# Gate and up products of a decoder's feed-forward: the high part of the weights meets both parts of x in one 512-column product

## Chip, core and metric

The kernel is one program on one NeuronCore of a Trainium2 chip. The metric is the time of one execution on the device in microseconds (us), lower is better. Engines are named as the profile names them: PE is TensorE's matmul, PEld its weight load, DVE is VectorE, ACT is ScalarE, POOL is GpSimd, SP is the queue that issues the DMAs.

## What is computed

Four decoder layers over 256 positions of width 1024. Each layer is a token mixer plus cross-attention, an output projection, a LayerNorm, and then a SwiGLU feed-forward of inner width 2816 with a second LayerNorm. The change is in the feed-forward alone:

```
def swiglu(x, w_gate_up, w_down):
    g, u = jnp.split(x @ w_gate_up, 2, axis=-1)
    return (jax.nn.silu(g) * u) @ w_down
...
        x = layer_norm(ALPHA * x + mixed, ln1_g[i], ln1_b[i])
        x = layer_norm(ALPHA * x + swiglu(x, w_gate_up[i], w_down[i]), ln2_g[i], ln2_b[i])
```

All inputs are float32.

## The kernel before

**Three products for one.** Each float32 operand is held as two parts of type fp32r: a high part (the value cast to fp32r) and a low part (the value minus its high part). A product of two operands is then the sum of high times high, high times low and low times high, all added into one PSUM bank. `mm3` issues these three matmuls (lines 256, 257 and 258), each with a weight load of its own (PEld).

**Weights.** They arrive in halves of 128 x 1024 float32 (512 KB) in the order of a plan. SP loads a half into one of four `raw` buffers (line 206), ACT casts it to the high part `wh` (line 214), DVE or POOL subtracts to the low part `wl` (line 230 or 228). In the feed-forward all but the first few low parts are DVE's. There are six pairs of `wh` and `wl`; a pair is free again once the last matmul that reads it is done, and a `raw` buffer once the low part is made.

**The feed-forward.** The 2816 inner columns are 22 blocks of 128. Blocks 0 and 1 are made another way (`a_mode`) and are not touched. Each of the other 20 is a *unit* in this text: `gu(i)` calls `t_mode`, which keeps the weights in the array and streams x transposed (`xT`, the high part `xh` and the low part `xl`, each 128 x 8 x 256). A unit uses two halves of weights; for the gate columns (`c` = 0) and then the up columns (`c` = 1) it runs 8 steps of k with `mm3`, so 2 x 8 x 3 = 48 matmuls of 256 columns. Gate and up lie side by side in one PSUM bank. Over four layers there are 80 units.

`t_task` reads the unit: silu of the gate on ACT (line 1057), times up on DVE (line 1059), the high part of the result `fth` on ACT (line 1061), the low part `ftl` on DVE (line 1063). It has three `sil` buffers to work in, one for a unit.

`down` multiplies the 128 positions of a row block with the rows of `w_down`: per block of inner columns 2 row blocks x 2 halves of columns x 3 matmuls of 512 columns, added into four PSUM banks that stay taken for the whole feed-forward. Four of the eight banks are left for units.

**Order.** PE's order is that of the program; the other engines' instructions are placed by a scheduler. In the middle of a feed-forward PE goes round a *period*: two units (block 2j+3, then 2j+4; called A and B here), then two blocks of `down` (2j+2 and 2j+3), 24 matmuls of 512 columns. So the first block of a `down` is the B of the period before, the second is this period's A. A period uses six halves of weights, two for A, two for B, one for each block of `down`, which is one round of the six pairs. At the end of a layer five units come one after another, then the last blocks of `down` (17 to 21 in `finish`), and the LayerNorm.

Of the kernel before, what the change touches and what calls it, by code (L numbers as in the profile page):

```python
# [10 lines left out]
F32R = mybir.dt.float32r  # L11
BF = mybir.dt.bfloat16
I32 = mybir.dt.int32
AF = mybir.ActivationFunctionType
OP = mybir.AluOpType
# [3 lines left out]
S = 256  # L19
# [19 lines left out]
def weight_plan():  # L39
    plan = []  # L40
    for l in range(DEPTH):
        kind = KINDS[l]
        v = [("v", l, i) for i in range(3)]
        qk = [("qk", l, i) for i in range(6)]
        if kind == 0:
            qi, qm = [("qi", l, 0), ("qi", l, 1)], ("qm", l, 0)
            if l:
                plan += [*qi, v[0], qk[0], qm, qk[1], v[1], qk[2], qk[3], qk[4], v[2], qk[5]]
            else:
                plan += [*qi, v[0], qm, qk[0], qk[1], v[1], qk[2], qk[3], qk[4], qk[5], v[2]]  # L50
                i = plan.index(MEM_AT)
                plan[i:i] = [("mk", 0, 0), ("mv", 0, 0)]
        elif kind == 1:
            plan += [v[0], qk[0], ("qm", l, 0), qk[2], v[1], qk[4], qk[1], qk[3], qk[5], v[2]]
        else:
            plan += [v[0], qk[0], ("qm", l, 0), qk[1], v[1], qk[2], qk[3], v[2], qk[4], qk[5]]
        plan += [("out", l, i) for i in (3, 0, 1, 2)]
        if l + 1 < DEPTH:
            plan += [("mk", l + 1, 0)]
        plan += [("gu", l, i) for i in range(3)]  # L60
        for j in range(NFF // 2):
            plan += [("dn", l, j)] + [("gu", l, i) for i in (2 * j + 3, 2 * j + 4) if i < NFF]
        plan.remove(("dn", l, NFF // 2 - 3))
        plan.remove(("dn", l, NFF // 2 - 2))
        i = plan.index(("dn", l, NFF // 2 - 1))
        plan[i:i] = [("dn", l, NFF // 2 - 3), ("dn", l, NFF // 2 - 2)]
        if l + 1 < DEPTH:
            plan += [("mv", l + 1, 0)]
    return plan
# [16 lines left out]
class Slots:  # L86
    def __init__(self, items):
        self.free = list(items)
# [24 lines left out]
class K:  # L113
    def __init__(self, tc, io, ctx):
        self.tc, self.nc, self.io = tc, tc.nc, io
        pool = lambda n: ctx.enter_context(tc.tile_pool(name=n, bufs=1))
        self.sb = pool("sb")
        self.pp = ctx.enter_context(tc.tile_pool(name="ps", bufs=1, space=bass.MemoryType.PSUM))

        ctx.enter_context(tc.manual_schedule(engines={mybir.EngineType.PE}))  # L120
        self.stalls = {}
        self.tasks = []
        T = self.t
        pair = lambda shp, tag, n: Slots([(T(shp, F32R, f"{tag}h{i}"), T(shp, F32R, f"{tag}l{i}")) for i in range(n)])
        one = lambda shp, tag, n, dt=F32: Slots([T(shp, dt, f"{tag}{i}") for i in range(n)])
        self.banks = Slots([self.pp.tile([128, 512], F32, name=f"bank{i}") for i in range(8)])
        self.raws = one([128, HALF], "raw", NR)
        self.cvs = pair([128, HALF], "w", NB)
        self.nats = one([128, 256], "nat", 3)
        self.qs = one([128, 2, 128], "q", 4, F32R)  # L130
        self.qms = one([128, 2, S], "qm", 2, F32R)
        self.es = {128: one([128, 2, 128], "e", 3), 256: one([128, 2, 256], "E", 3)}
        self.pTs = {1: pair([128, 1, 2, 128], "pa", 2), 2: pair([128, 2, 2, 128], "pb", 2)}
        self.vs = pair([128, 2, 256], "v", 3)
        self.fts = pair([128, S], "ft", 8)
        self.sils = one([128, S], "sil", 3)
        self.kks = one([128, 2, 2, S], "k", NKB, F32R)
        self.sts = one([128, 64], "st", 12)
        self.xT = (T([128, 8, S], F32R, "xh"), T([128, 8, S], F32R, "xl"))
        self.memT = (T([128, 8, S], F32R, "mh"), T([128, 8, S], F32R, "ml"))  # L140
        self.mk = [T([128, 2, 2, S], F32R, f"mk{i}") for i in range(2)]
        self.mv = (T([128, 2, 256], F32R, "mvh"), T([128, 2, 256], F32R, "mvl"))
        self.x = [T([128, D], F32, f"x{tb}") for tb in range(2)]
        self.lng, self.lnb = T([128, D], F32, "lng"), T([128, D], F32, "lnb")
        self.plan = weight_plan()
        self.hv = parts(self.plan)
        self.h0 = {}
        for i, (n, h, _) in enumerate(self.hv):
            if h == 0:
                self.h0[self.plan[n]] = i  # L150
        self.raw, self.cv = {}, {}
        self.n_raw = self.n_hi = self.n_lo = 0
        self.edge = False
# [137 lines left out]
    def t_mode(self, xT, key):  # L291
        b = self.take(self.banks, "bank")
        p = b.rearrange("p (c t) -> p c t", c=2)
        for c in range(2):
            for k in range(8):
                w = self.half(key, k // 4)
                cs = slice((k % 4) * 256 + c * 128, (k % 4) * 256 + c * 128 + 128)
                self.mm3(p[:, c], (w[0][:, cs], w[1][:, cs]), (xT[0][:, k], xT[1][:, k]), k == 0, k == 7)
                if k % 4 == 3:
                    if c:  # L300
                        self.free_half(key, k // 4)
                    if not (c and k == 7):
                        self.tick()
        return b, p

    def down(self, accs, what, l, kb, tb, ft, first):
        ts = slice(tb * 128, tb * 128 + 128)
# [727 lines left out]
    def ffn(self, l, ts):  # L1035
        nc = self.nc
        fts = [None] * NFF
        for i in range(N_AMODE):
            fts[i] = self.take(self.fts, "ft")
        gut = {}  # L1040

        def a_task(i, tb, b):
            s = yield from self.tk(self.sils)
            nc.scalar.activation(s[:, 0:128], b[:, 0:128], AF.Silu)
            nc.vector.tensor_tensor(s[:, 0:128], s[:, 0:128], b[:, 128:256], op=OP.mult)
            self.banks.put(b)
            yield W_A
            q = yield from self.tk(self.banks)
            nc.tensor.transpose(q[:, 0:128], s[:, 0:128], self.ident)
            t = slice(tb * 128, tb * 128 + 128)  # L1050
            self.split((fts[i][0][:, t], fts[i][1][:, t], q[:, 0:128], None))
            self.banks.put(q)
            self.sils.put(s)

        def t_task(i, b, p):
            s = yield from self.tk(self.sils)
            nc.scalar.activation(s, p[:, 0], AF.Silu)
            yield 1
            nc.vector.tensor_tensor(s, s, p[:, 1], op=OP.mult)  # L1059
            self.banks.put(b)  # L1060
            nc.scalar.copy(fts[i][0], s)  # L1061
            yield 1
            nc.vector.tensor_tensor(fts[i][1], s, fts[i][0], op=OP.subtract)
            self.sils.put(s)

        for tb in range(2):
            self.join(ts[tb])
            for i in range(N_AMODE):
                b = self.a_mode(self.xT, tb, ("gu", l, i), tb == 1)
                gut[i, tb] = self.spawn(a_task(i, tb, b))  # L1070
                self.tick()
        accs = self.new_accs()
        self.edge = False
        self.ln_params("ln2", l)

        def gu(i):
            b, p = self.t_mode(self.xT, ("gu", l, i))
            fts[i] = self.take(self.fts, "ft")
            gut[i, 0] = gut[i, 1] = self.spawn(t_task(i, b, p))
            self.tick()  # L1080

        def ready(kb, tb):
            self.join(gut[kb, tb])

        stop = NFF - HOLD_DN
        for what, _, i in [p for p in self.plan if p[1] == l and p[0] in ("gu", "dn")]:
            if what == "gu":
                if i >= N_AMODE:
                    gu(i)
                continue  # L1090
            for kb in (2 * i, 2 * i + 1):
                if kb < stop:
                    for tb in range(2):
                        ready(kb, tb)
                        self.down(accs, "dn", l, kb, tb, fts[kb], kb == 0)
                    self.fts.put(fts[kb])
        ts = self.finish(accs, "dn", l, range(stop, NFF), fts, ready, False, l == DEPTH - 1)
        for f in fts[stop:]:
            self.fts.put(f)
        return ts  # L1100
# [100 lines left out]
```

## Time and profile before

| | |
|---|---|
| median of 3 runs | 1353.04 us (1347.6 to 1353.33) |
| the profiled execution | 1351.82 us, span of its trace 1350.0 us, mean granted clock 0.983 |
| PE busy | 1287.3 us (95% of the span), 9186 matmuls |
| DVE busy | 897.5 us (66%) |
| ACT busy | 762.9 us (57%) |
| POOL busy | 316.4 us (23%) |
| read from memory | 223.02 MB, 166 GB/s over the span |

The span runs from the first to the last instruction in the trace; 1.82 us of the profiled execution lie outside it. Busy times of matmuls overlap on PE (each lasts longer than the distance to the next), so a busy PE says that it had work, and the distance from start to start says how fast it went.

### The profile page before, as it was taken

To read this page: it belongs to the slowest core of one execution; us is meant where nothing else is said; L and a number is where in the kernel's file an instruction comes from. 1 tells how busy PE (TensorE), PEld (TensorE's weight loads), DVE (VectorE), ACT (ScalarE), POOL (GpSimd) and SP (SyncE) were. 2 spreads that over 40 slices of the span, in tenths; PEclk is the share of its full clock that TensorE was granted. 3 is DMA by queue.
4 is the path that set the end of the run, shared out by engine and by line. 5 is a ranking of instruction groups with operands and counts; after the bars stand their busy time and mean duration, and the time that the engine had idled before them with its cause. 6 is when DMAs were issued, how large, how long until landed. Compare 5 with 4: busy or idle time off the path is not lost. (4 is left out here: it accounts for less than half of the span.)

```text
span 1350.0 us, 24249 instructions
## 1 busy us (share of the span) xinstructions
PE 1287.3 (95%) x9186; PEld 1212.5 (90%) x9186; DVE 897.5 (66%) x1940; ACT 762.9 (57%) x1512; POOL 316.4 (23%) x277
## 2 busy tenths in 40 slices
PE   6889899999999789999999999999999899999997
PEld 5879799999999779999989989999999898899996
DVE  7887775555578886555567877555568997655555
ACT  5668754444469745444447986444445897544441
POOL 3434440000045343000034444000014533300000
PEclk9989999999999889999999999999999999999999
DMA  8443356556564136565545345666546333655551
GB/s 300 126 149 110 110 180 199 187 188 184 170 203 150 70 103 240 185 189 180 183 155 180 133 141 169 206 185 188 186 138 218 127 125 126 203 188 188 187 176 59
DMA packets 63190, 225.65 MB, mean 167 GB/s; under 512 B 7776, under 2 KB 7776, under 8 KB 63072
## 3 DMA queue, kind: packets, MB, share of 16 engines
q1 hardware_dynamic: 62784, 224.10, 50.2%
q8 instruction: 72, 1.18, 0.4%
q14 instruction: 46, 0.38, 0.1%
q10 hardware_dynamic: 288, 0.00, 0.0%
HBM read 223.02 MB, written 1.05 MB: 166 GB/s over the span
## 5 line engine op out<-in xcount | busy, mean ns | idle before, releaser
L214 ACT CAST wh<-raw 128x1024 fp32r<-128x1024 f32 (+1 forms) x402 | 420.8, 1048 | 318.6 <-PE bank L257 177.2
L230 DVE TENSOR_TENSOR wl<-raw,wh 128x1024 fp32r<-128x1024 f32 (+1 forms) x294 | 378.2, 1288 | 273.9 <-ACT wh L214 269.1
L228 POOL TENSOR_TENSOR wl<-raw,wh 128x512 fp32r<-128x512 f32 x216 | 296.7, 1399 | 727.7 <-ACT wh L214 718.2
L256 PE MATMUL bank<-xh,wh 128*128 128x256 f32 x1344 | 382.1, 284 | 0.0
L257 PE MATMUL bank<-xl,wh 128*128 128x256 f32 x1344 | 381.2, 284 | 0.0
L258 PE MATMUL bank<-xh,wl 128*128 128x256 f32 x1344 | 381.2, 284 | 0.0
L257 PEld LDWEIGHTS bank<-xl,wh 128*128 128x128 f32 x1344 | 258.6, 192 | 1.2
L256 PEld LDWEIGHTS bank<-xh,wh 128*128 128x128 f32 x1344 | 258.6, 192 | 1.3
L258 PEld LDWEIGHTS bank<-xh,wl 128*128 128x128 f32 x1344 | 258.5, 192 | 0.0
L256 PE MATMUL bank<-wh,xh 128*128 128x256 f32 (+1 forms) x768 | 228.5, 298 | 2.8 <-ACT wh L214 1.9
L257 PE MATMUL bank<-wl,xh 128*128 128x256 f32 (+1 forms) x768 | 221.6, 289 | 2.5 <-DVE wl L230 2.3
L258 PE MATMUL bank<-wh,xl 128*128 128x256 f32 (+1 forms) x768 | 221.7, 289 | 0.8 <-DVE xl L270 0.6
L256 PE MATMUL bank<-wh,fth 128*128 128x512 f32 x480 | 189.8, 395 | 0.4 <-ACT fth L265 0.4
L257 PE MATMUL bank<-wl,fth 128*128 128x512 f32 x480 | 188.2, 392 | 0.0
L258 PE MATMUL bank<-wh,ftl 128*128 128x512 f32 x480 | 188.0, 392 | 0.0
L256 PEld LDWEIGHTS bank<-wh,xh 128*128 128x128 f32 x768 | 150.1, 196 | 4.0 <-ACT wh L214 2.4
L257 PEld LDWEIGHTS bank<-wl,xh 128*128 128x128 f32 x768 | 150.1, 195 | 3.1 <-DVE wl L230 3.1
L258 PEld LDWEIGHTS bank<-wh,xl 128*128 128x128 f32 x768 | 149.9, 195 | 1.7 <-DVE xl L270 1.7
L258 PEld LDWEIGHTS bank<-wh,ftl 128*128 128x128 f32 x480 | 90.5, 189 | 19.9 <-DVE ftl L270 0.7
L256 PEld LDWEIGHTS bank<-wh,fth 128*128 128x128 f32 x480 | 90.7, 189 | 17.5 <-ACT fth L265 0.8
L257 PEld LDWEIGHTS bank<-wl,fth 128*128 128x128 f32 x480 | 90.7, 189 | 16.3
L1061 ACT CAST fth<-sil 128x256 fp32r<-128x256 f32 x80 | 32.5, 406 | 107.3 <-DVE sil L1059 107.3
(194 smaller groups left out, 1553.0 us busy)
## 6 DMA issues: line engine op xcount, KB each, us to landing
raw<-in_w SPq DMA_DIRECT2D x396, 512.0 KB, 3.9
lng<-in_ln_g SPq DMA_DIRECT2D x8, 512.0 KB, 4.0
lnb<-in_ln_b SPq DMA_DIRECT2D x8, 512.0 KB, 6.2
raw<-in_w SPq DMA_DIRECT2D x4, 492.0 KB, 4.8
x<-in_xT SPq DMA_DIRECT2D x2, 512.0 KB, 5.4
E<-in_mem SPq DMA_DIRECT2D x4, 256.0 KB, 5.6
x<-in_x SPq DMA_DIRECT2D x2, 512.0 KB, 6.0
out_x<-x SPq DMA_DIRECT2D x4, 256.0 KB, 2.2
```

The costliest lines, as they stand in the source:

```text
L214: self.nc.scalar.copy(c[0][:, 0:wd], self.raw[n][:, 0:wd])
L228: self.nc.gpsimd.tensor_tensor(lo[:, c], r[:, c], hi[:, c], op=OP.subtract)
L230: self.nc.vector.tensor_tensor(lo[:, 0:wd], r[:, 0:wd], hi[:, 0:wd], op=OP.subtract)
L256: mm(out, lhsT=ah, rhs=bh, start=first, stop=False)
L257: mm(out, lhsT=ah, rhs=bl, start=False, stop=False)
L258: mm(out, lhsT=al, rhs=bh, start=False, stop=last)
L1061: nc.scalar.copy(fts[i][0], s)
```

## The change

The two parts of x now lie in one tile `x2`, 128 x 8 x 2 x 256, so that for each k the high part's 256 columns are followed by the low part's. `xT` names the two parts as slices of it for all other uses. A unit is made by `wide_mode` in place of `t_mode`: it takes two PSUM banks, one for gate and one for up. For each of them and each half of the weights it issues four matmuls of 512 columns, the weights' high part with both parts of x, and then four of 256 columns, the weights' low part with x's high part, into the first 256 columns of the bank. That is 2 x 2 x (4 + 4) = 32 matmuls in place of 48. The reader now has to add the two halves of each bank: an ACT copy of the second half, a DVE add of the first half to it, for gate and for up; then silu, the product and the two parts as before. A unit's reader takes two of the three `sil` buffers.

```
-        self.xT = (T([128, 8, S], F32R, "xh"), T([128, 8, S], F32R, "xl"))
+        self.x2 = T([128, 8, 2, S], F32R, "x2")
+        self.xT = (self.x2[:, :, 0], self.x2[:, :, 1])
...
+    def wide_mode(self, key):
...
+        mm = self.nc.tensor.matmul
+        bs = [self.take(self.banks, "bank") for _ in range(2)]
+        for c in range(2):
+            for h in range(2):
+                w = self.half(key, h)
+                cs = [slice(k * 256 + c * 128, k * 256 + c * 128 + 128) for k in range(4)]
+                for k in range(4):
+                    mm(bs[c], lhsT=w[0][:, cs[k]], rhs=self.x2[:, 4 * h + k].rearrange("p a t -> p (a t)"),
+                       start=h == k == 0, stop=False)
+                for k in range(4):
+                    mm(bs[c][:, 0:S], lhsT=w[1][:, cs[k]], rhs=self.x2[:, 4 * h + k, 0], start=False, stop=h == 1 and k == 3)
+                if c:
+                    self.free_half(key, h)
+                if not (c and h):
+                    self.tick()
+        return bs
...
-        def t_task(i, b, p):
+        def t_task(i, bs):
             s = yield from self.tk(self.sils)
-            nc.scalar.activation(s, p[:, 0], AF.Silu)
+            u = yield from self.tk(self.sils)
+            for d, b in ((s, bs[0]), (u, bs[1])):
+                nc.scalar.copy(d, b[:, S:2 * S])
+                nc.vector.tensor_tensor(d, b[:, 0:S], d, op=OP.add)
+                self.banks.put(b)
+            nc.scalar.activation(s, s, AF.Silu)
             yield 1
-            nc.vector.tensor_tensor(s, s, p[:, 1], op=OP.mult)
-            self.banks.put(b)
+            nc.vector.tensor_tensor(s, s, u, op=OP.mult)
+            self.sils.put(u)
             nc.scalar.copy(fts[i][0], s)
...
-            b, p = self.t_mode(self.xT, ("gu", l, i))
+            bs = self.wide_mode(("gu", l, i))
```

How the instructions stand on PE, in a unit of the first layer. First the kernel before, around the step from a unit's first half of weights (`wh_77`, `wl_78`) to its second (`wh_79`, `wl_80`); a row is one matmul with its output, its two inputs and its size:

```order
L256 MATMUL bank_65<-xh,wh_77 128x256
L257 MATMUL bank_65<-xl,wh_77 128x256
L258 MATMUL bank_65<-xh,wl_78 128x256
L256 MATMUL bank_65<-xh,wh_79 128x256
L257 MATMUL bank_65<-xl,wh_79 128x256
L258 MATMUL bank_65<-xh,wl_80 128x256
```

The same engine after the change, at the end of a `down` and through the first five groups of an A (x4 is four in a row; `x2` is printed as x_150):

```order
L257 MATMUL bank_64<-wh_83,fth_126 128x512
L258 MATMUL bank_64<-wl_84,fth_126 128x512
L259 MATMUL bank_64<-wh_83,ftl_127 128x512
L317 MATMUL bank_65<-x_150,wh_85 128x512 x4
L320 MATMUL bank_65<-x_150,wl_86 128x256 x4
L317 MATMUL bank_65<-x_150,wh_75 128x512 x4
L320 MATMUL bank_65<-x_150,wl_76 128x256 x4
L317 MATMUL bank_69<-x_150,wh_85 128x512 x4
```

Units and blocks of `down` follow one another as before; within a unit each high part of the weights is now loaded into the array once for both parts of x, and its low part is first read after four products.

ACT in one period of the first layer, before; the two readers are those of blocks 13 (its result `fth_126`) and 14 (`fth_128`):

```order
L214 CAST wh_81<-raw_72 128x1024
L214 CAST wh_83<-raw_73 128x1024
L214 CAST wh_85<-raw_74 128x1024
L214 CAST wh_75<-raw_71 128x1024
L1057 ACTIVATE sil_133<-bank_67 128x256
L1061 CAST fth_126<-sil_133 128x256
L214 CAST wh_77<-raw_72 128x1024
L214 CAST wh_79<-raw_73 128x1024
L1057 ACTIVATE sil_134<-bank_70 128x256
L1061 CAST fth_128<-sil_134 128x256
```

ACT in the same period after the change (gate banks 65 and 70, up banks 69 and 67):

```order
L1080 COPY sil_133<-bank_65 128x256
L1083 ACTIVATE sil_133<-sil_133 128x256
L215 CAST wh_85<-raw_74 128x1024
L215 CAST wh_75<-raw_71 128x1024
L1080 COPY sil_132<-bank_69 128x256
L1087 CAST fth_126<-sil_133 128x256
L1080 COPY sil_134<-bank_70 128x256
L215 CAST wh_77<-raw_72 128x1024
L1083 ACTIVATE sil_134<-sil_134 128x256
L215 CAST wh_79<-raw_73 128x1024
L1080 COPY sil_132<-bank_67 128x256
L1087 CAST fth_128<-sil_134 128x256
```

The six casts of the weights keep their order among themselves; the readers' pieces now stand between them, the gate's copy and silu ahead of the casts that follow its unit's weights, the up's copy behind them.

DVE at the same place after the change:

```order
L1081 TENSOR_TENSOR sil_133<-bank_65,sil_133 128x256
L231 TENSOR_TENSOR wl_86<-raw_74,wh_85 128x1024
L231 TENSOR_TENSOR wl_76<-raw_71,wh_75 128x1024
L1081 TENSOR_TENSOR sil_132<-bank_69,sil_132 128x256
L1085 TENSOR_TENSOR sil_133<-sil_133,sil_132 128x256
L1089 TENSOR_TENSOR ftl_127<-sil_133,fth_126 128x256
L1081 TENSOR_TENSOR sil_134<-bank_70,sil_134 128x256
```

The up's add stands behind the two subtractions of the weights that ACT casts ahead of the up's copy. Outside the units no engine's order differs from before, and POOL's and SP's rows are the same throughout.

## Rows read from the trace of the kernel before

**Rows 1.** Page, part 1: busy time, share of the span, instructions.

```profile
span 1350.0 us, 24249 instructions
...
PE 1287.3 (95%) x9186; PEld 1212.5 (90%) x9186; DVE 897.5 (66%) x1940; ACT 762.9 (57%) x1512; POOL 316.4 (23%) x277
```

**Rows 2.** Page, part 2: PE's granted clock in 40 slices of the span.

```profile
PEclk9989999999999889999999999999999999999999
```

**Rows 3.** Windows: the middle of each layer's feed-forward; columns in the first line.

```profile
core 0: us, PE busy (x) PEld busy (x) DVE busy (x) ACT busy (x) POOL busy (x), PEclk, DMA share, GB/s
205.00:320.00 115.00, 115.00 (x811) 108.32 (x810) 60.46 (x68) 51.57 (x68) 0.00 (x0) 1.00 0.59 191
545.00:660.00 115.00, 115.00 (x810) 108.32 (x809) 59.77 (x67) 51.72 (x68) 0.00 (x0) 1.00 0.59 187
860.00:975.00 115.00, 115.00 (x810) 108.31 (x809) 60.51 (x68) 51.54 (x68) 0.00 (x0) 1.00 0.59 185
1180.00:1290.00 110.00, 110.00 (x790) 104.27 (x789) 56.74 (x65) 48.43 (x65) 0.00 (x0) 1.00 0.57 185
```

**Rows 4.** Timeline of PE, first layer: start, duration, instruction; first matmuls of runs.

```profile
205.08 0.40 PE L256 MATMUL bank<-wh,fth 128*128 128x512 f32 x1
...
210.54 0.28 PE L256 MATMUL bank<-xh,wh 128*128 128x256 f32 x1
...
216.30 0.28 PE L256 MATMUL bank<-xh,wh 128*128 128x256 f32 x1
...
222.06 0.40 PE L256 MATMUL bank<-wh,fth 128*128 128x512 f32 x1
...
227.53 0.28 PE L256 MATMUL bank<-xh,wh 128*128 128x256 f32 x1
```

**Rows 5.** Groups by line and shape: count, busy us, mean ns, idle before.

```profile
L214 ACT CAST wh<-raw 128x1024 fp32r<-128x1024 f32 x396 | 415.3, 1050 | 317.4 <-PE bank L257 177.2 <-issue 75.9 <-PE bank L258 43.8
...
L230 DVE TENSOR_TENSOR wl<-raw,wh 128x1024 fp32r<-128x1024 f32 x290 | 372.9, 1287 | 273.6 <-ACT wh L214 268.8 <-PE bank L257 4.3
...
L1063 DVE TENSOR_TENSOR ftl<-sil,fth 128x256 fp32r<-128x256 f32 x80 | 34.0, 425 | 37.7 <-ACT fth L1061 37.7
L1059 DVE TENSOR_TENSOR sil<-sil,bank 128x256 f32<-128x256 f32 x80 | 33.1, 414 | 0.0
...
L1061 ACT CAST fth<-sil 128x256 fp32r<-128x256 f32 x80 | 32.5, 406 | 107.3 <-DVE sil L1059 107.3
...
L1057 ACT ACTIVATE sil<-bank 128x256 f32<-128x256 f32 x80 | 30.2, 378 | 0.0
...
L465 ACT COPY nat<-bank 128x256 f32<-128x256 f32 x56 | 20.6, 372 | 11.1 <-PE bank L258 8.5 <-DVE kn L675 2.1
```

**Rows 6.** Waits of all engines in 205 to 320: total us, times, longest.

```profile
ACT wh L214 <- PE bank L257: 30.1, 24, 3.1
ACT fth L1061 <- DVE sil L1059: 17.4, 13, 1.3
```

**Rows 7.** Timelines: PE's first `down` at 256, then ACT's and DVE's reader.

```profile
256.02 0.40 PE L256 MATMUL bank<-wh,fth 128*128 128x512 f32 x1
...
254.98 2.22 ACT L214 CAST wh<-raw 128x1024 fp32r<-128x1024 f32 x2 [1.52 <-PE bank L258]
257.10 0.38 ACT L1057 ACTIVATE sil<-bank 128x256 f32<-128x256 f32 x1
258.82 0.41 ACT L1061 CAST fth<-sil 128x256 fp32r<-128x256 f32 x1 [1.34 <-DVE sil L1059]
...
258.38 0.41 DVE L1059 TENSOR_TENSOR sil<-sil,bank 128x256 f32<-128x256 f32 x1
259.26 0.42 DVE L1063 TENSOR_TENSOR ftl<-sil,fth 128x256 fp32r<-128x256 f32 x1 [0.47 <-ACT fth L1061]
```

**Rows 8.** Page, part 6: the DMA of a half of weights: count, KB, us to landing.

```profile
raw<-in_w SPq DMA_DIRECT2D x396, 512.0 KB, 3.9
```

More of the change, by code (lines that the diff above doesn't have):

```diff
@@ L1076, in gu @@
         def gu(i):
-            b, p = self.t_mode(self.xT, ("gu", l, i))
+            bs = self.wide_mode(("gu", l, i))
             fts[i] = self.take(self.fts, "ft")
-            gut[i, 0] = gut[i, 1] = self.spawn(t_task(i, b, p))
+            gut[i, 0] = gut[i, 1] = self.spawn(t_task(i, bs))
             self.tick()
```

## The prediction

> **What bounds the kernel now.** I first read the busy shares [rows 1]: PE 95%, no other engine above 66%. The reader should not stop there, since PE's busy time counts matmuls that overlap. So next I read the feed-forward by itself, the only place that the change touches [rows 3]. In all four layers PE is busy for the whole of the stretch, at the full clock (1.00, which is 2.4 GHz), while ACT is busy for 51.6 of 115 us and DVE for 60.5. Then, whether PE in these stretches waits or only streams: the timeline of one period [rows 4]. A `down` of 24 matmuls of 512 columns begins at 205.08, unit A at 210.54, unit B at 216.30, the next `down` at 222.06, the next A at 227.53. That gives
>
> - 24 matmuls of 512 columns in 5.46 and 5.47 us: 227.5 to 227.9 ns each;
> - 96 matmuls of 256 columns in 11.52 us: 120.0 ns each, 5.76 us for a unit;
> - a period of 16.98 us with no room for a wait.
>
> So PE sets the pace of the feed-forward, by the distance between starts of matmuls. At 2.4 GHz 256 columns are 106.7 ns and 512 are 213.3 ns. What is left over is 13.3 ns for a product of 256 columns and 14.2 to 14.6 ns for one of 512: nearly the same for either, so it is a price of the product and not of its columns. That is what a change to fewer, wider products can earn.
>
> **The change, part by part.**
>
> *PE.* A unit streams as many columns as before (48 x 256 = 16 x 512 + 16 x 256). Before, it takes 48 x 120.0 = 5.76 us. After: 16 x 227.7 + 16 x 120.0 = 5.56 us. The gain is 16 x (240.0 - 227.7) = 197 ns, and over 80 units 15.7 us. Bounds: with 227.9 it is 15.5 us, with 227.5 16.0. The trace has no run of wide products with weights held and x streaming; the nearest are those of `down`, where the roles are the other way round but the type, the width and the weight load before every matmul are the same. I take their distance. If the wide products were paced 3% slower (234.5 ns) the gain would fall to 7 us; if they were 3% quicker (221 ns), it would be 24 us. I keep 7 and 24 as the ends of this term.
>
> A price per product of another size would change this. The trace shows 120.0 ns at 256 columns. The Trainium skill (TensorE: Matmul & The Clock Gate, section "Back-to-back issue gap") gives a warm distance of N / 2.4 + 2.5 ns, so 109.2 ns at 256 columns and 215.8 at 512. By it 16 products fewer are worth 40 ns a unit and 3.2 us in all, and the change would hardly be seen. The rows of this kernel differ from the page at both widths by 11 to 12 ns, and the measurement decides.
>
> *ACT and DVE.* A unit adds two ACT copies of 128 x 256 out of PSUM (nearest: 372 ns) and two DVE adds of that shape with one input in PSUM (nearest: line 1059, 414 ns) [rows 5]. Per period ACT has 6 casts of 1.05, and per unit 2 x 0.372 + 0.378 + 0.406, together 9.4 us of the new 16.6 us; DVE has 6 subtractions of 1.29 and per unit 3 x 0.414 + 0.425, together 11.1 us. In the run of five units at a layer's end the load is densest: per 5.56 us ACT 3.6 us, DVE 4.2 us. Neither engine is full, so the work is hidden under PE; without that cover it would be 80 x (0.744 + 0.828) = 126 us.
>
> *Lateness.* Both engines take their instructions in order, so more than the sum counts. I follow unit A after the change, from its first matmul at 0. The gate is done at 2.8; ACT copies it, DVE adds, ACT does silu, all by about 4.0. Next on ACT is the cast of a half of weights, into the pair that A releases after three quarters (4.2), done at 5.2, and then one into the pair that A's end (5.56) releases, done at 6.6. Only behind it stands the up's copy, done at 7.0. DVE subtracts those two halves until about 7.95, then add (8.4), product (8.8); ACT casts (9.2), DVE subtracts (9.7). The hand-over from one engine to the other costs some 0.03 us (in the reader of before, product until 258.79, cast at 258.82) [rows 7]. So A's result is there 4.1 us after A's end; the reader of before needs 3.7 us (from 256.02 to 259.68) [rows 7], so the longer chain is mostly paid for by starting the gate early. The result is wanted by the second block of the next `down`, which begins at 2 x 5.56 + 2.73 = 13.9: 4.2 us to spare. B's result has 11 us more. At the end of a layer the last unit's result is wanted by block 21 alone, behind 12 + 18 + 3 matmuls of 512 columns or 7.5 us: 3.4 us to spare.
>
> What waits behind the waiting instructions: B's gate copy and the four casts and subtractions after it. A cast waits for PE today already (30.1 us in 115) [rows 6], so ACT has that much idle time; a half is wanted a whole period after its cast, so 1 or 2 us there cost nothing. A `raw` buffer is then freed that much later, and its DMA from SP's queue lands 3.9 us after issue [rows 8] where four casts take 11 us: hidden too.
>
> *Banks.* A's two banks are written again two units and a `down` later at A's next turn; gate and up of B lie in the other two. A's up bank is read by 8.4, and its next use is at 16.6 + 2.8. Within the five units the third one wants the first one's gate bank at 11.1, long read. No wait for either.
>
> *`x2`.* Its writes and other reads keep their sizes, and each still waits for the same engines: 0.
>
> *Weights.* A period carries 6 x 512 KB in 16.6 instead of 16.98 us, 2% more than the 185 to 191 GB/s of rows 3, at a DMA share of 0.59: hidden.
>
> *The sum.* 1351.82 us of the profiled execution less 15.7 gives 1336.1; the median of the runs shown is 1.2 us above that execution, so from it 1337.3. I say **1337**. The runs of before lie from 1347.6 to 1353.3, so some 3 us either way is ordinary. Half a per cent, 6.8 us, is about what a measurement of this kernel can tell from no change.
>
> **The rivals.**
>
> *The price is not per product.* If, with x streaming, what is left over went with every 256 columns and not with the product, a wide product would take 240 ns, a unit 5.76 us as before, and the time would stay at 1353. Against it stand the two distances in rows 4, measured side by side: at 512 columns the rest is 14 ns, not 27. Chance 6%. By the Trainium skill's 2.5 ns (the page and section above) it would be 1350, which counts as the same case.
>
> *The reader comes too late (slower).* If A's result is more than 4.2 us later than worked out, PE waits at the second block of every `down`. The place would be ACT's queue, where the up's copy waits behind a cast, and that cast for PE or for a load. There are 7 periods in a layer, so 28 such places. From that point each further microsecond costs 28 us against 15.7 gained: at 1 us over, 1365. For it: ACT already waits 1.3 us for DVE in every reader [rows 6], and there are now two such waits. Against it: the room of 4.2 us is larger than everything that stands in front. Chance 6%.
>
> *A larger gain.* If four in a row of one shape run without the 13 ns, as columns alone would, a unit takes 16 x (213.3 + 106.7) = 5.12 us and the kernel gains 51 us: 1302. Against it: the 24 products of `down` are in a row too, and pay 14 ns. Chance 3%.
>
> *The forecast*, 15.7 us at 7 to 24 us: 85%.
>
> **How the numbers follow.** The forecast's own range from its bounds is 1353 - 24 to 1353 - 7, 1329 to 1346. Its ends are unlikely, since the nearest row is the same instruction, so I cut it to 1330 to 1345, which holds some 80% of the 85; the rivals lie outside, on both sides. Faster by over 0.5% means below 1346.3: the forecast and the larger gain, 88%. Within 0.5%: the first rival, 6%. Slower: the late reader, 6%.
>
> **What would show it.** In the middle of a layer's feed-forward the starts of a unit's 32 matmuls should lie 5.56 us from the next unit's, 228 ns after wide and 120 ns after narrow ones, `down` as before, and PE without idle time in the windows of rows 3. PE should have 9186 - 1280 = 7906 matmuls. ACT should have 160 more instructions of about 0.37 us, DVE 160 more of about 0.41, with longer waits of ACT for DVE at the new silu and cast. The sum is wrong if the wide ones are paced otherwise than 228 ns, or if PE shows waits for `fth`, `ftl`, `wh` or `wl` in those windows; the first changes the size of the gain, the second can turn its sign. A change in the slices of clock below 9 outside the feed-forward [rows 2] would be of another cause.

## The result and the profile after

The changed kernel takes 1344.78 us (median of 10 runs), the kernel before 1353.57 (10 runs): a ratio of 0.9928 with a 95% interval of 0.9908 to 0.9949, or 9.7 us less (7 to 12). One of the ten runs took 3094 us and is left out of the ratio and of all that is compared below (without it the median is 1344.33); nothing like it came in six further runs. The direction and the range of the prediction hold (1330 to 1345, barely); the size is some 60% of the 15.7 us that were forecast. The profiled execution took 1342.04 us, 9.8 less than that of before.

The page of the changed kernel, part 1, against [rows 1]:

```profile
span 1340.2 us, 22098 instructions
...
PE 1276.5 (95%) x7906; PEld 1143.9 (85%) x7906; DVE 959.8 (72%) x2100; ACT 812.3 (61%) x1672; POOL 316.2 (24%) x277
```

PE has 1280 matmuls fewer, ACT and DVE 160 instructions more each, as the prediction said. The windows in the middle of the feed-forwards, against [rows 3]:

```profile
205.00:320.00 115.00, 115.00 (x608) 98.66 (x607) 72.09 (x97) 60.22 (x96) 0.00 (x0) 1.00 0.60 195
545.00:660.00 115.00, 115.00 (x610) 98.73 (x609) 71.14 (x98) 60.81 (x97) 0.00 (x0) 1.00 0.59 191
```

PE is still busy throughout at the full clock. DVE rose from 60.5 to 72.1 us of 115, ACT from 51.6 to 60.2, and neither is near full. In the list of waits of PE and PEld from 205 to 355 there is not one row. So nothing new makes PE wait there, and what is missing of the gain inside the feed-forward must lie in PE's pace. The timeline of PE in the first layer (start, duration, line, shape, count), against [rows 4]:

```profile
205.43 0.40 PE L257 MATMUL bank<-wh,fth 128*128 128x512 f32 x1
...
210.90 1.07 PE L317 MATMUL bank<-x,wh 128*128 128x512 f32 x4
211.81 0.64 PE L320 MATMUL bank<-x,wl 128*128 128x256 f32 x4
212.28 1.09 PE L317 MATMUL bank<-x,wh 128*128 128x512 f32 x4
213.21 0.63 PE L320 MATMUL bank<-x,wl 128*128 128x256 f32 x4
213.68 1.09 PE L317 MATMUL bank<-x,wh 128*128 128x512 f32 x4
...
216.49 1.09 PE L317 MATMUL bank<-x,wh 128*128 128x512 f32 x4
...
222.10 0.40 PE L257 MATMUL bank<-wh,fth 128*128 128x512 f32 x1
...
355.75 0.40 PE L257 MATMUL bank<-wh,fth 128*128 128x512 f32 x1
```

Read the distances between starts. Four wide products straight after a `down` take 211.81 - 210.90 = 0.91 us, 228 ns each, as forecast. Four wide products after narrow ones take 0.93 (212.28 to 213.21), 232 ns each. Four narrow ones take 0.47, 118 ns each, a little less than 120. A and B together take 222.10 - 210.90 = 11.20 us, 5.60 a unit where 5.56 was forecast and 5.76 stood before.

A longer stretch gives the gain of a unit without rounding: from the first `down` of the layer to the first after the five last units, 150.32 us (205.43 to 355.75), with 19 units in it. The kernel before:

```profile
358.20 0.40 PE L256 MATMUL bank<-wh,fth 128*128 128x512 f32 x1
```

From 205.08 [rows 4] that is 153.12 us. So 2.80 us less for 19 units, 147 ns a unit, 11.8 us for 80. The `down`s lie inside this stretch, so what the change does to them is counted with the units. The same stretch in the other three layers is as long, to 0.02 us, in both traces. In the two profiled executions 9.8 us arrived; 2.0 us went in the stretches between the feed-forwards.

### The profile page after: what moved, and what is told of

It reads as the page before. It is cut to its first block, busy times and chain, and to the rows that moved or that the text cites. A ratio compares the mean times of both kernels' runs of the same rounds, so it can differ in the third digit from the quotient of the medians.

```text
span 1340.2 us, 22098 instructions
## 1 busy us (share of the span) xinstructions
PE 1276.5 (95%) x7906; PEld 1143.9 (85%) x7906; DVE 959.8 (72%) x2100; ACT 812.3 (61%) x1672; POOL 316.2 (24%) x277
## 5 line engine op out<-in xcount | busy, mean ns | idle before, releaser
L317 PE MATMUL bank<-x,wh 128*128 128x512 f32 x1280 | 349.4, 394 | 0.0
L317 PEld LDWEIGHTS bank<-x,wh 128*128 128x128 f32 x1280 | 221.0, 189 | 31.4
L257 PE MATMUL bank<-wh,x 128*128 128x256 f32 (+1 forms) x768 | 229.1, 298 | 2.9 <-ACT wh L215 1.9
L258 PE MATMUL bank<-wl,x 128*128 128x256 f32 (+1 forms) x768 | 221.9, 289 | 2.2 <-DVE wl L231 2.1
L259 PE MATMUL bank<-wh,x 128*128 128x256 f32 (+1 forms) x768 | 221.9, 289 | 1.1 <-DVE x L271 0.9
L320 PEld LDWEIGHTS bank<-x,wl 128*128 128x128 f32 x1280 | 196.2, 189 | 27.1
L320 PE MATMUL bank<-x,wl 128*128 128x256 f32 x1280 | 203.4, 281 | 0.0
L257 PEld LDWEIGHTS bank<-wh,x 128*128 128x128 f32 x768 | 150.7, 196 | 4.3 <-ACT wh L215 2.7
L258 PEld LDWEIGHTS bank<-wl,x 128*128 128x128 f32 x768 | 150.6, 196 | 2.9 <-DVE wl L231 2.9
L259 PEld LDWEIGHTS bank<-wh,x 128*128 128x128 f32 x768 | 150.3, 196 | 1.9 <-DVE x L271 1.9
L1080 ACT COPY sil<-bank 128x256 f32<-128x256 f32 x160 | 58.5, 366 | 61.4 <-PE bank L320 61.4
L1081 DVE TENSOR_TENSOR sil<-bank,sil 128x256 f32<-128x256 f32 x160 | 67.0, 419 | 31.0 <-ACT sil L1080 31.0
```

The costliest lines, as they stand in the source:

```text
L257: mm(out, lhsT=ah, rhs=bh, start=first, stop=False)
L258: mm(out, lhsT=ah, rhs=bl, start=False, stop=False)
L259: mm(out, lhsT=al, rhs=bh, start=False, stop=last)
L317: mm(bs[c], lhsT=w[0][:, cs[k]], rhs=self.x2[:, 4 * h + k].rearrange("p a t -> p (a t)"), start=h == k == 0, stop=False)
L320: mm(bs[c][:, 0:S], lhsT=w[1][:, cs[k]], rhs=self.x2[:, 4 * h + k, 0], start=False, stop=h == 1 and k == 3)
L1080: nc.scalar.copy(d, b[:, S:2 * S])
```

## The experiments

**The theory.** A wide product that follows narrow ones is slow, and the wide ones need some four or five in a row to come back to 227 ns. The change puts four such steps into every unit. **Rival 1**: a wide product with x streaming costs 232 ns wherever it stands. **Rival 2**: the reader's extra work on ACT and DVE slows PE.

**Only the reader and the layout** (e1_narrow): `x2`, two banks and the new reader, but the high part of the weights meets each part of x in a product of its own.

```
-                for k in range(4):
-                    mm(bs[c], lhsT=w[0][:, cs[k]], rhs=self.x2[:, 4 * h + k].rearrange("p a t -> p (a t)"),
-                       start=h == k == 0, stop=False)
+                for k in range(4):
+                    for part in range(2):
+                        mm(bs[c][:, part * S:part * S + S], lhsT=w[0][:, cs[k]], rhs=self.x2[:, 4 * h + k, part],
+                           start=h == k == part == 0, stop=False)
```

Expected: 

> The tile x2, the two banks and the new reader of the change, but 48 products of 256 columns a unit, as before the change. Theory (the missing part of the gain is a price of going from narrow to wide products, paid over the first four or five wide ones): no wide product, so 48 x 120 = 5.76 us a unit and the time of the kernel before, 1353 within 4. Rival 1 (a wide product with x streaming costs 232 ns wherever it stands): the same, 1353. Rival 2 (the reader's extra work slows PE by some 4 ns for every 512 columns or makes it wait): a unit of 5.83 us and some 5 us more than before, 1358.

Measured: 1354.38 us against 1353.44, ratio 1.0006 (0.9992 to 1.0021). Its first window:

```profile
205.00:320.00 115.00, 115.00 (x810) 108.29 (x809) 70.93 (x95) 59.33 (x94) 0.00 (x0) 1.00 0.59 192
```

The two ends of its stretch, from PE's timeline:

```profile
204.87 0.40 PE L257 MATMUL bank<-wh,fth 128*128 128x512 f32 x1
...
357.99 0.40 PE L257 MATMUL bank<-wh,fth 128*128 128x512 f32 x1
```

ACT and DVE carry the whole of the new reader (59.3 and 70.9 us), and the stretch is 153.12 us, as before to the hundredth. The reader costs nothing: rival 2 falls.

**Only the products** (e2_short_reader): the change's products with a reader of the old length. It leaves out the copies and the adds, and with them the product with the low part of x.

```
-            u = yield from self.tk(self.sils)
-            for d, b in ((s, bs[0]), (u, bs[1])):
-                nc.scalar.copy(d, b[:, S:2 * S])
-                nc.vector.tensor_tensor(d, b[:, 0:S], d, op=OP.add)
-                self.banks.put(b)
-            nc.scalar.activation(s, s, AF.Silu)
+            nc.scalar.activation(s, bs[0][:, 0:S], AF.Silu)
+            self.banks.put(bs[0])
...
-            nc.vector.tensor_tensor(s, s, u, op=OP.mult)
-            self.sils.put(u)
+            nc.vector.tensor_tensor(s, s, bs[1][:, 0:S], op=OP.mult)
+            self.banks.put(bs[1])
```

Expected: 

> The products of the change, with a reader of the old length: it leaves out the two copies and the two adds, so the product with the low part of x is dropped from the result. Theory and rival 1: PE's distances stay, a unit of 5.60 us and the time of the changed kernel, 1344 within 4. Rival 2 (the reader slows PE): wide products at 227 ns, a unit of 5.56 us, 1341 or below, and fewer waits.

Measured: 1343.69 us, ratio 0.9935 (0.9914 to 0.9957), the same as the changed kernel. Its first window, the two ends of its stretch, and four wide products that follow narrow ones:

```profile
205.00:320.00 115.00, 115.00 (x607) 98.57 (x606) 59.09 (x70) 54.11 (x69) 0.00 (x0) 1.00 0.60 196
...
204.98 0.40 PE L257 MATMUL bank<-wh,fth 128*128 128x512 f32 x1
...
211.83 1.09 PE L317 MATMUL bank<-x,wh 128*128 128x512 f32 x4
212.76 0.63 PE L320 MATMUL bank<-x,wl 128*128 128x256 f32 x4
...
355.30 0.40 PE L257 MATMUL bank<-wh,fth 128*128 128x512 f32 x1
```

The stretch is 150.32 us, that of the changed kernel to the hundredth. The distances of 232 ns (0.93 us for four) are there with a light reader too.

**All products wide** (e6_all_wide): the low part of the weights also meets both parts of x, which adds the product of the two low parts.

```
-                for k in range(4):
-                    mm(bs[c][:, 0:S], lhsT=w[1][:, cs[k]], rhs=self.x2[:, 4 * h + k, 0], start=False, stop=h == 1 and k == 3)
+                for i in range(2):
+                    for k in range(4):
+                        mm(bs[c], lhsT=w[i][:, cs[k]], rhs=self.x2[:, 4 * h + k].rearrange("p a t -> p (a t)"),
+                           start=h == k == i == 0, stop=h == i == 1 and k == 3)
```

Expected: 

> All 32 products of a unit 512 columns wide: the low part of the weights meets both parts of x as well (the product of the two low parts is added, which the other kernels leave out). No narrow product stands in the middle of a feed-forward. Theory: 227 ns each, 7.26 us a unit, 80 x 1.66 = 133 us more than the changed kernel, 1477. Rival 1: 232 ns each, 7.42 us, 1490. Were the low part's products slow or quick for their own sake, the two groups of four would differ.

Measured: 1476.92 us, ratio 1.092 (1.0886 to 1.0954); the theory said 1477. PE's timeline of an A and a B:

```profile
213.79 1.07 PE L318 MATMUL bank<-x,wh 128*128 128x512 f32 x4
214.70 1.07 PE L318 MATMUL bank<-x,wl 128*128 128x512 f32 x4
...
227.40 1.07 PE L318 MATMUL bank<-x,wl 128*128 128x512 f32 x4
228.30 0.39 PE L257 MATMUL bank<-wh,fth 128*128 128x512 f32 x1
```

64 products from 213.79 to 228.30 are 226.7 ns each, with x streaming and the same reader. Rival 1 falls: with no narrow product about, the same wide ones run at 227 ns.

**Sixteen and sixteen** (e4_sixteen): the same 32 products, all wide ones of a unit first (gate, up), then all narrow ones.

```
+        for c in range(2):
+            for h in range(2):
+                for k in range(4):
+                    mm(bs[c], lhsT=self.half(key, h)[0][:, k * 256 + c * 128:k * 256 + c * 128 + 128],
+                       rhs=self.x2[:, 4 * h + k].rearrange("p a t -> p (a t)"), start=h == k == 0, stop=False)
+            self.tick()
+        for c in range(2):
+            for h in range(2):
+                for k in range(4):
+                    mm(bs[c][:, 0:S], lhsT=self.half(key, h)[1][:, k * 256 + c * 128:k * 256 + c * 128 + 128],
+                       rhs=self.x2[:, 4 * h + k, 0], start=False, stop=h == 1 and k == 3)
...
```

Expected: 

> The same 32 products a unit, in another order: sixteen wide ones (gate, then up), then sixteen narrow ones. Theory: one step from narrow to wide in a unit in place of four; wide ones start at 235, 233, 236, 228, 231 and then run at 227, narrow ones at 119.5, so 1163 + 11 x 227 + 16 x 119.5 = 5.57 us a unit against 5.60, about 2.5 us less in all: 1342. Rival 1: wide ones at 232 throughout, 5.60 us, 1344. For both the gate is done 1.9 us later in its unit; if that made the result late, PE would wait for fth or ftl in the second block of a down.

Measured: 1336.83 us, ratio 0.9886 (0.9871 to 0.9900). PE's timeline of an A and a B:

```profile
210.83 3.79 PE L315 MATMUL bank<-x,wh 128*128 128x512 f32 x16
214.46 2.08 PE L321 MATMUL bank<-x,wl 128*128 128x256 f32 x16
216.37 3.82 PE L315 MATMUL bank<-x,wh 128*128 128x512 f32 x16
220.02 2.08 PE L321 MATMUL bank<-x,wl 128*128 128x256 f32 x16
221.94 0.40 PE L257 MATMUL bank<-wh,fth 128*128 128x512 f32 x1
```

In B sixteen wide ones after narrow ones take 3.65 us, 228.1 ns each; in A, after a `down`, 3.63, 226.9. The unit is 5.55 us. Its stretch is 149.29 us (205.36 to 354.65), and in its list of waits of PE from 205 to 355 there is no row: the gate comes some 1.8 us later, and the reader is still in time. The time is 5 us below the 1342 that were expected; the stretch accounts for 4.3 us less than the changed kernel where 2.5 were expected.

A second time beside the changed kernel on the same chip (after_again, e4_again). Expected of the changed kernel: 

> The changed kernel once more, beside the order with sixteen. Its units are 5.60 us long in every run, so the feed-forwards give back 11.7 us. Theory: what its median lacks of that is time between the feed-forwards, which differs from run to run; with more runs it comes out at 1342 to 1345. A rival that the change itself makes the stretches between longer would have all runs at 1344 or more.

Expected of sixteen and sixteen: 

> Sixteen wide and then sixteen narrow products, once more on the same chip as the changed kernel. By the lengths of the feed-forwards (154.95 against 156.01 us) it should be 4.2 us quicker than the changed kernel; the first runs said 7.

Measured: the changed kernel 1343.76 us, ratio 0.9923 (0.9907 to 0.9940); sixteen and sixteen 1336.91, ratio 0.9880 (0.9861 to 0.9898). The stretches are 150.31 and 149.29 us, as in the first runs. The difference of the medians is again 7 us, of which the feed-forwards explain 4.3 (16.1 less 11.8). The two pairs of profiled executions differ by 4.2 (1342.04, 1337.82) and 4.5 us (1340.94, 1336.46), as the stretches say; what else is in the 7 us is not shown.

**One and one** (e3_alternate): wide and narrow in turn, so that every wide product but the first behind a `down` follows a narrow one.

```
-                for k in range(4):
                     mm(bs[c][:, 0:S], lhsT=w[1][:, cs[k]], rhs=self.x2[:, 4 * h + k, 0], start=False, stop=h == 1 and k == 3)
```

Expected: 

> The same 32 products a unit, one wide and one narrow in turn. Theory, if one narrow product is enough for the full price of the next wide one: 235 + 117 = 352 a pair, 5.63 us a unit, 2.4 us more than the changed kernel in all. If the price grows with the number of narrow ones before, the wide ones stay nearer to 227 and the unit is 5.50 to 5.60 us.

Measured: 1346.08 us, ratio 0.9943 (0.9927 to 0.9959). PE's timeline:

```profile
210.91 0.39 PE L317 MATMUL bank<-x,wh 128*128 128x512 f32 x1
211.14 0.28 PE L319 MATMUL bank<-x,wl 128*128 128x256 f32 x1
211.25 0.40 PE L317 MATMUL bank<-x,wh 128*128 128x512 f32 x1
211.48 0.28 PE L319 MATMUL bank<-x,wl 128*128 128x256 f32 x1
211.60 0.40 PE L317 MATMUL bank<-x,wh 128*128 128x512 f32 x1
...
222.20 0.40 PE L257 MATMUL bank<-wh,fth 128*128 128x512 f32 x1
```

A and B take 11.29 us: 5.64 a unit, 353 ns a pair where 352 were expected; in long runs of their own a wide and a narrow one are 347 together. One narrow product is enough to make the next wide one slow. The stretch is 151.27 us (205.44 to 356.71).

**Eight and eight** (e5_eight): as sixteen and sixteen, but gate is finished (eight wide, eight narrow) before up begins. The edit is against sixteen and sixteen.

```
             self.tick()
-        for c in range(2):
             for h in range(2):
                 for k in range(4):
```

Expected: 

> Eight wide and then eight narrow products for gate, the same for up: two steps from narrow to wide in a unit in place of four. Theory: eight wide ones 233 + 235 + 228 + 232 + 230 + 3 x 227 = 1839, eight narrow ones 113 + 119 + 6 x 120 = 952, so 5.58 us a unit, between the changed kernel's 5.60 and the 5.55 of sixteen; 1.6 us less than the changed kernel.

Measured: 1339.89 us, ratio 0.9910 (0.9883 to 0.9937). Its A and B in PE's timeline:

```profile
212.00 1.98 PE L315 MATMUL bank<-x,wh 128*128 128x512 f32 x8
...
223.15 0.40 PE L257 MATMUL bank<-wh,fth 128*128 128x512 f32 x1
```

A and B take 11.15 us, the stretch 149.67 (206.53 to 356.20).

All together, by the length of a run of one width. The gain by the stretch is the difference to 153.12, over 19 units, times 80; the gain by the medians is the median time of the kernel before less that of this one, timed together (two kernels were timed twice):

| products in a run | A and B, us | stretch, us | gain by the stretch, us | gain by the medians, us |
|---|---|---|---|---|
| 48 narrow (e1) | 11.52 | 153.12 | 0 | -0.9 |
| 1 wide, 1 narrow (e3) | 11.29 | 151.27 | 7.8 | 7.2 |
| 4 and 4 (the change) | 11.20 | 150.32 | 11.8 | 9.2 and 9.5 |
| 8 and 8 (e5) | 11.15 | 149.67 | 14.5 | 13.4 |
| 16 and 16 (e4) | 11.11 | 149.29 | 16.1 | 16.6 and 16.4 |

The same 32 products a unit give between 7.8 and 16.1 us by their order, and in none of these runs does the list of waits of PE from 205 to 355 have a row. That is the theory, shown, with one thing to add: how long the slow start lasts. It is five products behind a long run of narrow ones; behind the changed kernel's units, which end in four narrow ones, the `down` that begins at 222.10 needs nine:

```profile
224.19 0.39 PE L257 MATMUL bank<-wh,fth 128*128 128x512 f32 x1
...
227.36 0.39 PE L259 MATMUL bank<-wh,ftl 128*128 128x512 f32 x1
```

Its first nine take 2.09 us, 232 ns each, the next fourteen 3.17, 226 each.

## Why the prediction was right, and where its size was off

*What bounds.* Right. PE's pace set the feed-forward before and after, with no wait of PE in either; a reader with twice the instructions on ACT and DVE cost 0.00 us in the stretch (e1).

*The price of a product.* Right as a mechanism: at full clock a product of either width costs some 13 ns above its columns (226.7 and 120.0 ns in long runs, less 213.3 and 106.7), and fewer products are faster. Every product here has a weight load of its own, so no run tells the price of the product from that of its load. Sixteen fewer a unit earn 16.1 us where the runs are long; the forecast was 15.7. The rival in which the rest goes with the columns gives nothing and is out. So is the 2.5 ns of the Trainium skill (TensorE: Matmul & The Clock Gate, section "Back-to-back issue gap"), which the page gives for an isolated product and by which, as an estimate, the change would have earned 3.2 us: no long run here came so near to the columns at the full clock; the least are 226.7 ns at 512 columns and 120 at 256.

*The step that failed* is the term "16 x 227.7": "I take their distance", the mean over a `down`'s 24 products, used for runs of four. The mean hid a slow start, and the slow start was in the trace of before. Two more rows of PE's timeline of the kernel before show it:

```profile
206.24 0.39 PE L258 MATMUL bank<-wh,ftl 128*128 128x512 f32 x1
...
210.32 0.39 PE L258 MATMUL bank<-wh,ftl 128*128 128x512 f32 x1
```

The `down` begins at 205.08 [rows 4], behind narrow products. Its first five take 206.24 - 205.08 = 1.16 us, 232 ns each; the eighteen from there to 210.32 take 4.08 us, 226.7 each. So the rest of 14.2 to 14.6 ns that the prediction read at 512 columns was 13.4 ns and the slow start. In a run of 24 the slow start adds 1 ns to the mean; in runs of four it is nearly the whole run. Narrow products after wide ones are a little quicker (118 for 120), which gives some of it back. The term measured 147 ns a unit in place of 197, 11.8 us in place of 15.7. A small part of that is the `down`s, put at "as before": with the longer slow start their products take 228.5 ns in the mean where they took 227.8.

*The rest.* The measured times show 9 to 10 us, some 2 less than the stretches; the interval of either measurement (7 to 12 and 8 to 13 us) holds 11.8. A second profiled execution of the changed kernel has the stretch of the first to 0.01 us and took 1340.94 us: 10.9 us less than before, where the first took 9.8 less. So half of the 2 us came and went with no change of the kernel. Between the feed-forwards PE's granted clock falls to half (1.2 GHz) at times that are not the same in every execution (it is 0.96 on average from 360 to 520 us of the changed kernel, 0.95 there with sixteen and sixteen). The whole of the span outside the four stretches is 737.6 us before, 738.9 and 737.7 in the two of the changed kernel, 738.6 and 737.2 in the two of sixteen and sixteen. The rival that the change itself makes these stretches longer was to show by all six further runs at 1344 us or more; four of them were below. A small effect of that kind is neither shown nor excluded.

*The reader in time.* Right. The timelines of ACT and DVE for an A that begins at 227.59:

```profile
230.62 0.37 ACT L1080 COPY sil<-bank 128x256 f32<-128x256 f32 x1 [1.74 <-PE bank L320]
231.48 0.42 ACT L1083 ACTIVATE sil<-sil 128x256 f32<-128x256 f32 x1 [0.49 <-DVE sil L1081]
231.81 2.15 ACT L215 CAST wh<-raw 128x1024 fp32r<-128x1024 f32 x2
233.86 0.36 ACT L1080 COPY sil<-bank 128x256 f32<-128x256 f32 x1
236.06 0.41 ACT L1087 CAST fth<-sil 128x256 fp32r<-128x256 f32 x1 [1.84 <-DVE sil L1085]
...
236.50 0.43 DVE L1089 TENSOR_TENSOR ftl<-sil,fth 128x256 fp32r<-128x256 f32 x1 [0.47 <-ACT fth L1087]
```

The up's copy stands behind the two casts, as worked out, and the result is there at 236.93, 9.3 us after the unit's start (forecast 9.7). It is wanted at about 227.59 + 2 x 5.6 + 2.73 = 241.5: 4.6 us to spare, where 4.2 were worked out. The late reader, the rival on the other side, did not come.

*Banks, layout and weights* at nothing: right. The banks and the layout are in e1, whose stretch is as before; the weights' faster rate is in the changed kernel, whose first window has 195 GB/s and no wait of PE.

## What to carry to other kernels

Where the matmul engine streams without a wait, look for a price per product above its columns (here 13 ns): joining two narrow products that share their stationary operand earns it. Then try keeping products of one width together: here the same instructions in runs of sixteen earned twice what they earned in turn. And before a mean distance is carried to another pattern, look at the first few distances of a run, not only at its first and last row.

## What was not expected of the hardware

At the full clock a 512-column product that follows a 256-column one starts a slow run: 232 ns on average over the first five behind a long run of narrow ones, 227 from there on, and nine slow ones behind units of four and four; a single 256-column product is enough to start it (353 ns a pair, in turn). It shows with either operand streaming (units, and `down`), and the part of the weights makes no difference (64 wide ones of both parts at 226.7). What in the engine does it, no run here shows.
